# Filler projections placed between the steps of the Gram products of a hybrid encoder on one Trainium2 core

## Chip, core and metric

The kernel runs on one core of one Trainium2 chip. Its time is the device time of one execution in microseconds (us). TensorE is called PE in the profile, VectorE DVE, ScalarE ACT, GpSimd POOL, and SP is the engine whose queue issues the DMAs.

## What is computed

A trunk of two layers on 1024 tokens of width 1024. The first layer normalises, projects into ten groups of columns, and feeds two mixers: A, a recurrence with decay (RWKV-7) of 8 heads of 64, and B, attention in chunks of 64 over the own and eight previous chunks, also 8 heads. Both are gated, joined and projected back. The second layer is a gated spatial mixing, and a normalisation ends it.

```python
def step(state, inp):                       # mixer A
    r_t, w_t, k_t, v_t, a_t, b_t = inp
    sa = jnp.einsum('bhvk,bhk->bhv', state, a_t)
    state = (state * w_t[:, :, None, :]
             + sa[..., None] * b_t[:, :, None, :]
             + v_t[..., None] * k_t[:, :, None, :])
    y_t = jnp.einsum('bhvk,bhk->bhv', state, r_t)
    return state, y_t
...
s = jnp.einsum('bhqd,bhkd->bhqk', q_blk, kb).astype(jnp.float32) * scale + bias    # mixer B
p = jax.nn.softmax(s, axis=-1)
return jnp.einsum('bhqk,bhkd->bhqd', p.astype(vb.dtype), vb)
...
y_a = rwkv7_mix(p_r, p_k, p_v, p_wd, p_ad, w0, w2, a0, a2, k_k, k_a, r_k, lnx_g, lnx_b)
y_a = y_a * jax.nn.silu(gate_a)
y_b = chunk_attention(q_b, k_b, v_b, att_bias) * jax.nn.silu(gate_b)
return h + jnp.concatenate([y_a, y_b], axis=-1) @ w_out
```

## The kernel before

All products are done in three passes of split numbers (high x high, high x low, low x high; lines 256, 258 and 260), so that the large projections dominate TensorE. One such matmul of 128 x 512 is called a filler here when it is issued through `Fill`.

The program goes through these stages, in order of time:

- Normalisation and the projections of mixer A (to about 265 us). Each ends with the decayed keys and queries stored to DRAM (`ar_d`, `bk_d`, `v_d`).
- The recurrence, in four quarters of 256 tokens, each of four chunks of 64. `stage_a` loads `bk`, `ag` and `uv`, and makes the Gram products: for two chunk groups (`cg`) and two pairs of heads (`pj`) it issues one group of matmuls into two PSUM tiles `psg` (line 713; pool `ps_m`, two buffers), which VectorE masks into `G` and `ag` (line 717), four evacuations for a group. Then `rest` scales `bk` on GpSimd and transposes it (`pst`, line 684) through the same two buffers. `stage_b` solves the triangular blocks, a chain on VectorE with small products `psx` (line 770). `stage_c` runs the state from chunk to chunk (`zz`, `yy`, `us`). `stage_d` normalises the output. The `bk` tile has one buffer, so the next load of it waits for the transposes of the one before.
- The attention of eight heads: `att_a` makes scores, `att_b` transposes the probabilities (`st`), splits them (`ph` on ScalarE, `pl` on VectorE) and multiplies with the values into `po`. A finished half of a pair of heads goes, times its gate, to `yb_d`.
- The second half of the output projection from `yb_d`, and then the second layer.

Fillers run through the recurrence and the attention. `early_steps` are the 16 projections of mixer B (q, k, v, gate for four pairs of heads), 48 matmuls each; behind them come `out_steps`, the half of the output projection that needs mixer A alone, 8 x 2 x 12 matmuls, whose weights `WHL` can only be loaded when the last early one is issued. `fill.pump(n, mark, low)` takes n such matmuls from this one sequence; what is left when the attention has been written runs behind it, by `run(fill.steps)`. The loops of the program set how many are asked for at each place: `QP` ahead of the first `stage_a`, `QB` between the quarters, `QC` in each chunk, `QA` and `FILLS` in the attention.

The order on each engine is set by a scheduler at build time, by priority. A filler has a priority lowered by `low` (400 for `QP` and `QB`), and `mark` only sets that it stands behind a certain instruction:

```python
def pump(self, n, mark, low=None):
    self.mark, self.fresh = mark, True
    with tc.high_priority(offset=-(self.low if low is None else low)):
        for _ in range(n):
            next(self.steps, None)
    self.mark = None
```

The engines' queues then run in that order, each instruction waiting for its own operands.

Of the kernel before, what the change touches and what calls it, by code (L numbers as in the profile page):

```python
# [52 lines left out]
YP = 1  # L53
LATE = 1
NPO = 1
QP = 84
FILLS = [5, 4, 4, 6, 4, 3, 3, 3]
QA = 14
QB = [80, 10, 10, 10]
QC = [[8, 8, 7], [8, 9, 7], [8, 8, 9], [8, 8, 7]]  # L60
W0SCALE = 0.6065306597126334

# [37 lines left out]
def trunk_kernel(  # L100
# [4 lines left out]
    nc = tc.nc  # L105
# [145 lines left out]
    fill = Fill()  # L251
# [131 lines left out]
    def proj_cm(*args, **kw):  # L383
        run(proj_steps(*args, **kw))
# [41 lines left out]
    def gate_evac(dst):  # L426

        def evac(ps, hf):
            gt = fl.tile([P, 2, 512], F32, tag="gt", name="gt", bufs=2)
            nc.scalar.activation(gt[:, 0], ps, AF.Tanh, scale=0.5)  # L430
            nc.vector.scalar_tensor_tensor(gt[:, 1], gt[:, 0], 1.0, ps, op0=ALU.add, op1=ALU.mult)
            nc.sync.dma_start(dst[:, hf * 512:hf * 512 + 512], gt[:, 1])
        return evac
# [105 lines left out]
    for p in range(NPAIR):  # L539
# [23 lines left out]
        for hf in range(2):  # L563
# [33 lines left out]
            bk = ra.tile([P, 8, P], F32, tag="bk", name="bk", bufs=2)  # L597
# [66 lines left out]
    hss = [slice(64 * h, 64 * h + 64) for h in range(2)]  # L664
    oss = hss[::-1]

    def stage_a(q):

        d = quart[q]
        d["ag"], d["g"], d["bt"], d["uv"] = [], [], [], []  # L670
        rq = (re_, rb)[q % 2]
        parts = []

        def rest(cg, bk, bt):

            c0 = 4 * q + 2 * cg
            for i in range(2):
                nc.gpsimd.tensor_tensor(
                    bk[:, :, i, :], bk[:, :, i, :], pcs[:, c0 + i, :].unsqueeze(2).to_broadcast([P, 4, P]), op=ALU.mult)
            for pj in range(2):  # L680
                pst = ps_m.tile([P, 4, P], F32, tag="m", name="pst")
                for j in range(2):
                    for i in range(2):
                        nc.tensor.transpose(pst[:, 2 * j + i], bk[:, 2 * pj + j, i, :], ident)
                nc.scalar.copy(bt[:, 2 * pj:2 * pj + 2].rearrange("p j i t -> p (j i) t"), pst)

        for cg in range(2):
            o = 4 * q + 2 * cg
            uv = rq.tile([P, 2, 4, P], F32, tag="uv", name="uv", bufs=2)

            ag = rq.tile([P, 2, 4, 2, P], F32, tag="ag", name="ag", bufs=2)
            bk = (rb if q == 0 and cg else re_).tile(
                [P, 4, 2, P], F32, tag="bt" if q == 0 and cg else "bk", name="bk", bufs=2 if q == 0 and cg else 1)
            nc.sync.dma_start(bk, bk_d[o // 8][:, :, o % 8:o % 8 + 2, :].rearrange("a p c t -> p a c t"))
            for h in range(2):
                nc.sync.dma_start(ag[hss[h], h], ar_d[o // 8][:, hss[h], o % 8:o % 8 + 2, :].rearrange("a p c t -> p a c t"))
            for i in range(2):
                for h in range(2):
                    nc.sync.dma_start(
                        uv[oss[h], i, :, hss[h]],  # L700
                        v_d[o // 8][:, 64 * (o % 8 + i):64 * (o % 8 + i) + 64, hss[h]].rearrange("a s n -> s a n"))
                    if q == cg == i == 0:
                        nc.gpsimd.memset(uv[hss[h], i, :, hss[h]], 0.0)
            if cg == 0:
                d["G"] = rq.tile([P, 2, 4, 2, P], F32, tag="G", name="G", bufs=1)
            g = d["G"][:, cg]
            bt = rq.tile([P, 4, 2, P], F32, tag="bt", name="bt", bufs=2)
            for pj in range(2):
                psg = [ps_m.tile([P, 4, P], F32, tag="m", name=f"psg{h}") for h in range(2)]
                for j in range(2):  # L710
                    for i in range(2):
                        for h in range(2):
                            nc.tensor.matmul(psg[h][:, 2 * j + i], lhsT=bk[hss[h], 2 * pj + j, i, :],  # L713
                                             rhs=ag[hss[h], h, 2 * pj + j, i, :], start=True, stop=True)
                for h in range(2):
                    for dst, r in ((g[:, 2 * pj:2 * pj + 2], hss[h]), (ag[:, h, 2 * pj:2 * pj + 2], oss[h])):
                        nc.vector.tensor_tensor(
                            dst[r].rearrange("p j i t -> p (j i) t"), psg[h][r],
                            gmask[r].unsqueeze(1).to_broadcast([64, 4, P]), op=ALU.mult)
            d["g"].append(g)  # L720
            d["ag"].append(ag)
            d["bt"].append(bt)
            d["uv"].append(uv)
            parts.append((cg, bk, bt))
            if q > 0:
                rest(*parts.pop())
        for a in parts:
            rest(*a)
# [190 lines left out]
    for p in range(NPAIR):  # L919
        proj_cm(w_in_e[0], 1664 + p * P, gate_evac(bg_d[p][1]))  # L920
    fill.pump(QP, mark, FLB)
    stage_a(0)
    mark = stage_b(0)
    stage_a(1)
    fill.pump(QB[0], mark, FLB)
    for q in range(3):
        stage_b(q + 1)
        mark = stage_c(q)
        if q < 2:
            stage_a(q + 2)  # L930
        fill.pump(QB[q + 1], mark, FLB)
        stage_d(q)
# [454 lines left out]
```

## Time and profile before

| | us |
|---|---|
| median of 3 timed runs | 1179.46 (1178.08 to 1182.88) |
| the profiled execution | 1180.27 |
| its span, first to last instruction | 1178.6 |
| TensorE busy | 1119.8 (95%) |
| VectorE, ScalarE, GpSimd busy | 622.6, 469.0, 432.0 |
| mean granted clock of TensorE, share of 2.4 GHz | 0.974 |

The busy time of TensorE is modelled from the starts of its matmuls, so a matmul that stands in the array longer than the next one needs shows as overlap, and a TensorE that works slowly also shows as busy. The granted clock says at which of its two levels, 1.2 or 2.4 GHz, it ran.

### The profile page before, as it was taken

The numbers are of one execution on the slowest core, as the hardware profiler recorded it, in microseconds if no ns is written. First come the engines' busy times: TensorE is split into PE (matmuls) and PEld (weight loads), VectorE is DVE, ScalarE is ACT, GpSimd is POOL, SyncE is SP. The second block draws the span as 40 slices with busy tenths as digits, with TensorE's granted clock in tenths as the row PEclk, the third lists the DMA queues.
The fourth block names the chain that finished last, engine by engine and source line by source line (L and its number), as shares of the span: only waits on it lengthen the run. The fifth ranks groups of instructions, "written<-read, shape, count | busy, mean of one in ns | idle before, by whom it ended". The sixth has DMA issues, their size and how long they took to land.

```text
span 1178.6 us, 21117 instructions
## 1 busy us (share of the span) xinstructions
PE 1119.8 (95%) x8162; PEld 929.2 (79%) x8162; DVE 622.6 (53%) x1276; ACT 469.0 (40%) x1008; POOL 432.0 (37%) x448
## 2 busy tenths in 40 slices
PE   8999999998899898999997899899999999999997
PEld 5788778787777676767886778789998888888886
DVE  6455656456585867634687767464100753333433
ACT  5554554430322232312675646234417232231432
POOL 4345545361223433423322463311402464351222
PEclk9999999995999998999999899999999999999999
DMA  6124446469322533293587784862401232122541
GB/s 209 39 81 143 116 117 164 140 205 193 109 83 83 161 101 100 73 215 118 162 227 184 222 264 147 270 216 90 134 10 55 87 110 72 63 88 89 166 133 71
DMA packets 169125, 156.39 MB, mean 133 GB/s; under 512 B 25257, under 2 KB 138562, under 8 KB 168898
## 3 DMA queue, kind: packets, MB, share of 16 engines
q1 hardware_dynamic: 169026, 155.06, 44.9%
q8 instruction: 64, 1.05, 0.4%
q14 instruction: 35, 0.29, 0.1%
HBM read 102.02 MB, written 53.00 MB: 132 GB/s over the span
## 4 chain that ended last, share of the span: by engine, by line
PE 58%; DMA 7%; DVE 5%; ACT 1%; issue 1%; POOL 1%; SPq 0%; DVEq 0%; ACTq 0%; POOLq 0%
PE acc L256 8%; PE acc L258 8%; PE acc L260 8%; PE accv L256 3%; PE accv L260 3%; PE accv L258 3%; PE accu L256 3%; PE accu L260 2%; PE accg L260 2%; PE accu L258 2%; PE accg L258 2%; PE accg L256 2%; PE st L1069 2%; DMA wraw<-in_w_out_e_dram 2%; PE psx L770 1%; PE psg L713 1%
## 5 line engine op out<-in xcount | busy, mean ns | idle before, releaser
L256 PE MATMUL acc<-xH,wh 128*128 128x512 f32 x528 | 214.7, 407 | 1.6 <-DVE rT L422 0.6
L258 PE MATMUL acc<-xL,wh 128*128 128x512 f32 x528 | 213.5, 405 | 0.0
L225 POOL TENSOR_TENSOR wl<-wraw,wh 128x512 fp32r<-128x512 f32 (+1 forms) x106 | 148.9, 1424 | 175.4 <-ACT wh L222 160.0
L260 PE MATMUL acc<-xH,wl 128*128 128x512 f32 x528 | 212.0, 401 | 0.0
L256 PEld LDWEIGHTS acc<-xH,wh 128*128 128x128 f32 x528 | 101.5, 192 | 23.6 <-DVE rT L422 1.0
L258 PEld LDWEIGHTS acc<-xL,wh 128*128 128x128 f32 x528 | 101.2, 192 | 21.2 <-issue 0.9
L260 PEld LDWEIGHTS acc<-xH,wl 128*128 128x128 f32 x528 | 101.0, 191 | 21.2
L256 PE MATMUL acc<-WHL,yh 128*128 128x512 f32 x256 | 101.9, 398 | 4.5 <-DVE res L1142 3.4
L222 ACT CAST wh<-wraw 128x512 fp32r<-128x512 f32 (+1 forms) x102 | 62.7, 653 | 108.5 <-PE acc L258 43.3
L258 PE MATMUL acc<-WHL,yh 128*128 128x512 f32 x256 | 100.8, 394 | 0.0
L260 PE MATMUL acc<-WHL,yl 128*128 128x512 f32 x256 | 100.8, 394 | 0.0
L256 PE MATMUL accv<-wh,xH 128*128 128x256 f32 x256 | 71.7, 283 | 0.0
L258 PE MATMUL accv<-wl,xH 128*128 128x256 f32 x256 | 71.7, 283 | 0.0
L260 PE MATMUL accv<-wh,xL 128*128 128x256 f32 x256 | 71.4, 285 | 0.0
L256 PEld LDWEIGHTS acc<-WHL,yh 128*128 128x128 f32 x256 | 48.4, 189 | 15.6 <-DVE res L1142 4.1
L258 PEld LDWEIGHTS acc<-WHL,yh 128*128 128x128 f32 x256 | 48.3, 189 | 9.6 <-POOL WHL L1114 0.2
L260 PEld LDWEIGHTS acc<-WHL,yl 128*128 128x128 f32 x256 | 48.1, 188 | 9.7
L256 PE MATMUL accu<-xH,wh 128*128 128x512 f32 x128 | 50.5, 395 | 0.0
L260 PE MATMUL accu<-xH,wl 128*128 128x512 f32 x128 | 49.9, 390 | 0.0
L258 PE MATMUL accu<-xL,wh 128*128 128x512 f32 x128 | 49.9, 390 | 0.0
L260 PE MATMUL accg<-xH,wl 128*128 128x512 f32 x128 | 49.9, 389 | 0.0
L256 PE MATMUL accg<-xH,wh 128*128 128x512 f32 x128 | 49.8, 389 | 0.0
(433 smaller groups left out, 2438.0 us busy)
## 6 DMA issues: line engine op xcount, KB each, us to landing
wraw<-in_w_in_e_dram SPq DMA_DIRECT2D x66, 256.0 KB
wraw<-in_w_in_o_dram SPq DMA_DIRECT2D x32, 256.0 KB
xt<-in_x_dram SPq DMA_DIRECT2D x8, 512.0 KB
ar_d<-ar SPq DMA_DIRECT2D x8, 512.0 KB
q_d<-hl SPq DMA_DIRECT2D x8, 512.0 KB
bk<-bk_d SPq DMA_DIRECT2D x8, 512.0 KB
ag<-ar_d SPq DMA_DIRECT2D x16, 256.0 KB
k_d<-hl SPq DMA_DIRECT2D x8, 512.0 KB
```

What stands on the lines that cost most here:

```text
L222: c_ = hi(wh[:, ks], raw)
L225: nc.gpsimd.tensor_tensor(wl[:, ks], raw, f32(wh[:, ks]), op=ALU.subtract)
L256: fill(nc.tensor.matmul(ps, lhsT=ah(k), rhs=bh(k), start=(k == 0), stop=False), k == 0)
L258: fill(nc.tensor.matmul(ps, lhsT=ah(k), rhs=bl(k), start=False, stop=False), False)
L260: fill(nc.tensor.matmul(ps, lhsT=al(k), rhs=bh(k), start=False, stop=(k == nk - 1)), False)
L713: nc.tensor.matmul(psg[h][:, 2 * j + i], lhsT=bk[hss[h], 2 * pj + j, i, :], rhs=ag[hss[h], h, 2 * pj + j, i, :], start=True, stop=True)
L770: nc.tensor.matmul(ps[t_, i], lhsT=lhsT(f, i), rhs=rhs[f[0], i], start=True, stop=True)
L1069: nc.tensor.transpose(st[:, o:o + P], pfs[j][:, k0:k0 + P], ident)
```

## The change

Each Gram group is followed by `QG` = 6 fillers at the priority of their place (`low` = 0), behind the last matmul of the group. There are four groups in each of the four `stage_a`. `QP` goes from 84 to 104, and the first of `QB` from 80 to 56. `QC`, `QA` and `FILLS` stay, and so does the sequence from which the fillers come.

```diff
-QP = 84
+QP = 104
+QG = 6
 FILLS = [5, 4, 4, 6, 4, 3, 3, 3]
 QA = 14
-QB = [80, 10, 10, 10]
+QB = [56, 10, 10, 10]
...
-                            nc.tensor.matmul(psg[h][:, 2 * j + i], lhsT=bk[hss[h], 2 * pj + j, i, :],
-                                             rhs=ag[hss[h], h, 2 * pj + j, i, :], start=True, stop=True)
+                            m_ = nc.tensor.matmul(psg[h][:, 2 * j + i], lhsT=bk[hss[h], 2 * pj + j, i, :],
+                                                  rhs=ag[hss[h], h, 2 * pj + j, i, :], start=True, stop=True)
+
+                fill.pump(QG, m_, 0)
```

The first place is TensorE's order at the first Gram stage, the last fillers ahead of it (`acc`) and its first groups, before:

```order
L258 MATMUL acc<-xL,wh 128x512
L260 MATMUL acc<-xH,wl 128x512
L713 MATMUL psg_2566<-ag,bk 128x128 x4
L713 MATMUL psg_2567<-ag,bk 128x128 x4
L713 MATMUL psg_2580<-ag,bk 128x128 x4
L814 MATMUL zz<-uv,ag 64x64
L817 MATMUL yy<-uv,ag 64x64
L713 MATMUL psg_2581<-ag,bk 128x128 x4
```

and of the change, where 20 more `acc` stand ahead of these rows:

```order
L259 MATMUL acc<-xL,wh 128x512
L714 MATMUL psg_2601<-ag,bk 128x128 x4
L714 MATMUL psg_2602<-ag,bk 128x128 x4
L261 MATMUL acc<-xH,wl 128x512
L257 MATMUL acc<-xH,wh 128x512
L259 MATMUL acc<-xL,wh 128x512
L261 MATMUL acc<-xH,wl 128x512
L257 MATMUL acc<-xH,wh 128x512
L259 MATMUL acc<-xL,wh 128x512
L714 MATMUL psg_2621<-ag,bk 128x128 x4
L817 MATMUL zz<-uv,ag 64x64
L820 MATMUL yy<-uv,ag 64x64
```

Six fillers have moved between the first group and the second; 6 and 4 more follow in the same way behind the second and the third.

The second place is TensorE's order where the second Gram stage begins. Before, the first 8 transposes `pst` of the first stage are followed by 17 fillers, 8 more transposes and 19 fillers, of which the last stand here ahead of the second stage's first group:

```order
L256 MATMUL acc<-xH,wh 128x512
L258 MATMUL acc<-xL,wh 128x512
L260 MATMUL acc<-xH,wl 128x512
L713 MATMUL psg_2933<-ag,bk 128x128 x2
L713 MATMUL psg_2934<-ag,bk 128x128 x2
```

and of the change:

```order
L257 MATMUL acc<-xH,wh 128x512
L259 MATMUL acc<-xL,wh 128x512
L685 MATMUL pst<-ident,bk 128x128 x16
L714 MATMUL psg_3004<-ag,bk 128x128
L714 MATMUL psg_3005<-ag,bk 128x128
```

All 16 transposes now stand together, directly ahead of the group, and the fillers stand ahead of them.

The third place is the end of the attention on TensorE, the last products `po` of the last head. Before, fillers (`acc<-WHL`) stand between them, and 49 more behind the last one:

```order
L1074 MATMUL po<-ph,vb 128x384
L1074 MATMUL po<-ph,vb 128x128
L260 MATMUL acc<-WHL,yl 128x512
L256 MATMUL acc<-WHL,yh 128x512
L258 MATMUL acc<-WHL,yh 128x512
L1076 MATMUL po<-pl,vb 128x384
L1076 MATMUL po<-pl,vb 128x128
```

and of the change, where the `acc` that follow are the projection from `yb_d`:

```order
L1077 MATMUL po<-ph,vb 128x384
L1077 MATMUL po<-ph,vb 128x128
L1079 MATMUL po<-pl,vb 128x384
L1079 MATMUL po<-pl,vb 128x128
L257 MATMUL acc<-WHL,yh 128x512
L259 MATMUL acc<-WHL,yh 128x512
```

The last filler of the sequence stands early in the products of the seventh head now.

## Rows read from the trace of the kernel before

**Rows 1.** The page: TensorE's busy time, its slices, and its granted clock in tenths.

```profile
PE 1119.8 (95%) x8162; PEld 929.2 (79%) x8162; DVE 622.6 (53%) x1276; ACT 469.0 (40%) x1008; POOL 432.0 (37%) x448
...
PE   8999999998899898999997899899999999999997
...
PEclk9999999995999998999999899999999999999999
```

**Rows 2.** Stretches: length, then PE, PEld, DVE, ACT, POOL, PEclk, DMA share, GB/s.

```profile
265.00:270.00 5.00, 1.15 (x9) 0.78 (x7) 0.00 (x0) 0.00 (x0) 0.01 (x1) 1.00 1.19 253
270.00:294.00 24.00, 22.75 (x112) 19.49 (x111) 17.25 (x29) 1.23 (x3) 4.08 (x4) 0.50 0.90 186
294.00:334.00 40.00, 36.71 (x583) 29.66 (x581) 26.43 (x53) 13.23 (x26) 10.75 (x12) 0.96 0.28 88
334.00:541.00 207.00, 191.52 (x2934) 150.15 (x2935) 131.54 (x291) 58.50 (x124) 74.55 (x86) 0.96 0.45 125
...
629.00:672.00 43.00, 34.21 (x185) 28.77 (x183) 30.55 (x84) 27.34 (x76) 18.41 (x18) 0.88 0.82 219
...
700.00:723.00 23.00, 20.61 (x119) 17.04 (x117) 16.85 (x47) 13.50 (x38) 10.12 (x10) 1.00 0.62 196
723.00:737.00 14.00, 13.46 (x79) 11.22 (x78) 9.77 (x22) 7.12 (x18) 4.63 (x5) 1.00 0.44 135
737.00:750.00 13.00, 13.00 (x58) 10.42 (x56) 3.46 (x6) 1.07 (x2) 2.54 (x2) 1.00 0.79 256
750.00:755.00 5.00, 1.80 (x9) 1.49 (x9) 2.54 (x2) 2.17 (x3) 4.32 (x2) 1.00 0.46 136
```

**Rows 3.** TensorE's timeline: start, duration, line, tiles, form, count [idle before <-releaser].

```profile
264.56 0.39 PE L256 MATMUL acc<-xH,wh 128*128 128x512 f32 x1
...
265.02 0.39 PE L260 MATMUL acc<-xH,wl 128*128 128x512 f32 x1
269.25 4.93 PE L713 MATMUL psg<-ag,bk 64*128 64x128 f32 x24 [3.85 <-DMA ag<-ar_d]
...
288.05 1.12 PE L684 MATMUL pst<-ident,bk 128*128 128x128 f32 x4 [0.68 <-ACT bt L685]
...
300.55 1.17 PE L713 MATMUL psg<-ag,bk 64*128 64x128 f32 x16
```

**Rows 4.** VectorE's timeline, first and last of 16 evacuations of the first stage.

```profile
270.60 0.68 DVE L717 TENSOR_TENSOR G<-psg,gmask 64x512 f32<-64x512 f32 x1 [6.50 <-PE psg L713]
...
289.04 0.68 DVE L717 TENSOR_TENSOR ag<-psg,gmask 64x512 f32<-64x512 f32 x1
```

**Rows 5.** The chain that ended last: start, us, what.

```profile
319.26 4.30 DMA bk<-bk_d
...
403.06 6.90 DMA bk<-bk_d
...
421.89 0.62 PE zz L814 x16
422.50 0.47 PE yy L817 x16
```

**Rows 6.** Stretches of tile acc alone: PE, PEld, DVE, ACT, PEclk, DMA share, GB/s.

```profile
270.00:294.00 24.00, 5.18 (x12) 4.18 (x13) 0.00 (x0) 0.00 (x0) 0.50 0.90 186
...
700.00:723.00 23.00, 10.88 (x40) 6.60 (x38) 3.44 (x5) 0.00 (x0) 1.00 0.62 196
723.00:737.00 14.00, 7.47 (x26) 4.47 (x27) 1.27 (x2) 0.00 (x0) 1.00 0.44 135
```

**Rows 7.** Timelines of VectorE and TensorE at the end of the attention.

```profile
729.72 0.68 DVE L1083 TENSOR_TENSOR yb<-po,lo 64x512 f32<-64x512 f32 x1
...
735.70 0.39 PE L1076 MATMUL po<-pl,vb 128*128 128x384 f32 x2
...
742.50 0.69 DVE L1127 TENSOR_TENSOR yl<-yraw,yh 128x512 fp32r<-128x512 f32 x1
...
752.46 0.69 DVE L1142 TENSOR_TENSOR res<-acc,res 128x512 f32<-128x512 f32 x1 [7.16 <-DMA res<-in_x_dram]
```

## The prediction

> **What bounds the kernel now.** I read the page first. TensorE is busy 95% of the span, and its digits stand at 8 or 9 in nearly every slice; the granted clock has one bad slice, the tenth [rows 1]. So the time is TensorE's work at full clock plus what it loses to waits and to half clock, and since the change adds and removes no matmul, only the lost part can change. The next view is a table of stretches, cut where the program changes its stage [rows 2]. The reader is to see four things in it. In 265 to 270 TensorE works 1.15 us of 5. In 270 to 294 it looks busy (22.75 of 24), but at clock 0.50. From 294 to 541, the recurrence with its fillers, it stands idle 3.3 + 15.5 us at clock 0.96. And in 629 to 672 it is idle 8.8 us: there the last projection has been issued, and the next kind of filler still waits for its weights.
>
> What happens in 265 to 294 is in the timelines [rows 3, 4]. The last filler starts at 265.02, TensorE waits 3.85 us for the first ag load, and then the Gram products run between VectorE's evacuations: 16 of them, the first at 270.60, the last at 289.04, each 0.68 us. Two PSUM buffers mean that TensorE can be only one pair ahead. It is busy in pieces and at half clock for all of that.
>
> **The first Gram stage.** Prices at full clock: two fillers start 0.46 us apart, so one costs 0.23 us; 16 Gram records take 1.17 us; 16 zz records 0.62 and 16 yy records 0.47 [rows 3, 5]. From 265.4 to 294.0, 28.6 us, TensorE did 64 Gram records (4.7), 32 records of zz and yy (1.1), 8 transposes (two fours of 1.12 at half clock, so 1.1 together at full) and 12 fillers (2.8) [rows 3, 6]: 9.7 us of work, 18.9 lost. After the change 20 fillers (4.6 us) cover the 3.85 us wait. Then the order puts 6, 6 and 4 fillers between the Gram pairs: 3.7 us, beside 4.7 + 1.1 of its own work, is 9.5 us in the 16 x 0.68 = 11 us that VectorE needs. Nothing here should hold the clock down. I leave 3.5 us lost (1.5 of pacing, 2 for the last two PSUM buffers, which VectorE frees only after two transposes of its own). **Gain 15.4 us.** The bounds are 18.9 (nothing lost) and 3.85 (only the load wait goes, the clock stays low).
>
> Of the queues: the fillers taken early are the end of a k projection and most of a v projection, whose weights ACT and POOL split, in both orders, ahead of the first Gram stage; their evacuations, stores and the weight loads behind them move forward with them. SP's order up to the last load of the first stage is the same row for row, so no Gram load is late for that reason; behind it two weight loads and one vb_d store now stand ahead of the reload that comes next.
>
> **What the move uncovers.** The second Gram stage must reload the one bk buffer, which the transposes of the first free. Before, the order has 36 fillers between those transposes and the next Gram pair: 36 x 0.23 = 8.3 us, longer than the reload, which takes 4.30 us in one row and 6.90 in another [rows 5]. After, the 16 transposes stand directly ahead of the next pair, and ahead of the third group of that stage it is so again. TensorE's queue is in order, so nothing passes: each time it waits for the DMA less what is left of the transposes (some 1 us). I take 3.5 us each, **7 us**, nearer the 4.30 row, since the DMA share falls from 0.90 to 0.28 there [rows 2]. Bounds: 0 if VectorE is late anyway, and 13.8 (2 x 6.90).
>
> **The other stages.** The budget of early fillers changes thus: ahead of the first stage 84 to 104; in each of four Gram stages 4 x 6 = 24 new; after the second Gram stage 80 to 56. That is 20 + 96 - 24 = 92 more before the attention, 48 of them in the third and fourth Gram stages, 48 x 0.23 = 11 us, in a stretch that loses 15.5 us idle and, at clock 0.96, some 8 us more (8% of 207 us at half) [rows 2]. If they fall into those waits the stretch stays as long and 11 us of work is done in it for nothing; if the chain of evacuation, solve and state is pushed along by them, nothing is won. I take just over the middle, **6 us gained**; bounds 0 and 11.
>
> **The attention pays.** There are 960 filler steps (16 projections x 48, and 8 x 2 x 12 of the first half of the output projection). Up to the attention 574 were asked for, now 666; the attention asks for 332. Before, 54 were left and ran behind it: that is why 737 to 750 is busy 13 of 13 [rows 2]. After, the fillers end 38 early, and the order confirms it: behind the start of the seventh head's products no filler stands until the last po. TensorE has 92 x 0.23 = 21 us less to do there, but loses cover:
> - Seventh head (700 to 723): 40 fillers (9.2 us) and 2.4 idle leave 11.4 us of its own work. VectorE is busy 16.85, of which 5 adds of 0.69 belong to the fillers: 13.4. Without fillers VectorE and its waits set about 15.5 us. Lost 4 where 2.4 were lost: +2.
> - Last head (723 to 737): 26 fillers (6 us) and 0.5 idle leave 7.5; the chain of transposes, copy, subtract and product needs about 9.5: +1.5.
> - Handover: the last head's first half is added at 729.72; its product with the gate, the store, the reload and the split, 742.50 to 743.2, follow [rows 7]. Some 3 us of these 13.5 I put down to queueing behind other work, so the chain needs about 10, and the second half of the head, 6 us with fillers (to the last po at 735.70), then takes some 4. Six us stay open. Before, the 54 leftovers covered it, and what stayed open was one wait of 3.2 us (750 to 755), for a residual load that blocked VectorE until 752.46 [rows 2, 7]: +2.5 net.
>
> **6 us lost** in sum; bounds 2 (VectorE's own time falls with the fillers' traffic gone) and 16 (the half clock below).
>
> **Sum.** -15.4 + 7 - 6 + 6 = -8.4 us. The profiled execution took 1180.3 us, its span 1178.6; the three timed runs have a median of 1179.46. 1179.5 - 8.4 = **1171 us**, -0.7%.
>
> **The rivals.**
> 1. *All of it is won.* The reload is back in time because VectorE's evacuations are late anyway, and the other stages take their 48 fillers into waits: -18 - 10 + 8 = -20, so 1160. For it: 18.8 us idle between 294 and 541 [rows 2], more than the fillers need. Against it: in the order nothing at all stands between the transposes and the pair that needs the reload.
> 2. *No change.* The start wins only its 3.85 us wait and part of the clock, 8 to 10 us, the reload takes 7 back, and the attention's open end the rest: 1178 to 1181. For it: fillers are only moved, and their work was already done at full speed where it stood (13 of 13 busy).
> 3. *Slower: the uncovered heads fall to half clock.* In 629 to 672, where fillers were short before, the clock is 0.88 with TensorE busy 34 of 43, so mostly it held; but in 270 to 294 it stayed at 0.50 [rows 2]. If the last two heads run at 1.2 GHz, their own 11.4 + 7.5 us become 38 instead of the 25 of my forecast: +13, and the two heads that run short of fillers at the beginning of the attention add 3: 1171 + 16 = 1187. It decides once the low level holds through both of the last heads.
>
> The Trainium skill's page "TensorE: Matmul & The Clock Gate" speaks for the third rival in its section "Why this matters for your kernels": idle gaps between bursts of matmuls bring the array back to half rate, so bursts should follow each other directly. Here 265 to 294 agrees (3.85 us of waiting, then 0.50). By that rule the first stage is cured, and the last heads become the next such place, 1187; the 0.88 of 629 to 672 makes me hold this the less likely.
>
> **How the numbers follow.** About 0.5% (6 us) is what a measurement of this kernel tells from no change. My forecast, by its own terms 1164 to 1179: 0.48. First rival 0.18, second 0.19, third 0.15. Faster: rival 1 and about 0.7 of the forecast, 0.52. Same: the rest of the forecast and most of rival 2, 0.30. Slower: rival 3 and a little of rival 2, 0.18. The range that holds 8 in 10 reaches to most of rival 1 and to the edge of rival 3: 1157 to 1186.
>
> **What would show it.** Right: no wait for ag at 265, clock 1.00 through 270 to 285, a wait of 3 to 5 us of TensorE for bk near 290 and another some 15 us later, no acc row among the last head's products, a gap of 4 to 7 us after the last po, and attention done some 15 us earlier relative to its start. Wrong: low clock still in the first Gram stage (then it is not the gap that sets it); no wait for bk (rival 1); the stretch of the recurrence longer by 10 us (its chain is pushed); or low clock through the last heads (rival 3).

## The result, and the profile after

The changed kernel took 1188.38 us (median of six runs, 1187.12 to 1190.1) against 1179.96 us of the kernel before on the same chip (1178.08 to 1182.88): ratio 1.007, 95% interval 1.0054 to 1.0086. It is slower by 0.7%, where the forecast was 0.7% faster. The profiled execution took 1187.37 us, its span is 1185.7. All line numbers behind the Gram products are 3 higher now.

The page, TensorE's busy time, its slices and its granted clock, to be read against [rows 1]:

```profile
PE 1119.7 (94%) x8162; PEld 924.9 (78%) x8162; DVE 616.4 (52%) x1276; ACT 470.2 (40%) x1008; POOL 432.9 (37%) x448
...
PE   7999999998889989999987999899999999999997
...
PEclk8999999998789989999998999999999999999999
```

The one bad slice of the clock has gone (its 5 is an 8), and two weak ones, 7 and 8, stand behind it. The table of stretches says where (columns as in [rows 2]); the last three rows are the heads that run short of fillers, most of the last two heads, and the handover from the attention to the projection behind it:

```profile
265.00:270.00 5.00, 5.00 (x24) 3.92 (x23) 0.57 (x1) 1.64 (x3) 1.54 (x2) 1.00 1.18 249
270.00:283.00 13.00, 13.00 (x112) 10.56 (x110) 8.99 (x15) 0.00 (x0) 3.02 (x3) 1.00 1.13 211
283.00:300.00 17.00, 10.63 (x48) 8.56 (x47) 12.34 (x29) 3.53 (x6) 2.04 (x2) 0.69 0.64 191
300.00:320.00 20.00, 15.12 (x197) 11.16 (x195) 11.91 (x26) 4.21 (x8) 4.97 (x6) 0.75 0.13 41
320.00:340.00 20.00, 15.80 (x247) 12.88 (x247) 17.18 (x45) 5.28 (x11) 3.28 (x4) 0.83 0.23 73
340.00:358.50 18.50, 18.50 (x439) 14.65 (x438) 6.73 (x11) 6.78 (x15) 5.18 (x8) 1.00 0.25 83
...
600.00:643.00 43.00, 32.95 (x187) 27.20 (x185) 30.33 (x90) 27.46 (x75) 16.94 (x17) 0.92 0.82 210
...
734.00:752.70 18.70, 16.68 (x109) 13.93 (x106) 16.46 (x45) 14.35 (x37) 2.55 (x2) 1.00 0.30 102
752.70:757.00 4.30, 0.54 (x3) 0.30 (x3) 1.03 (x2) 1.37 (x3) 2.53 (x2) 1.00 0.51 151
```

From 265 to 283 TensorE is busy all the time at full clock, where it waited and then ran at half clock before [rows 2]. From 283 to 340 it stands idle 6.4 + 4.9 + 4.2 = 15.5 us, and the clock takes 17 x 0.31 + 20 x 0.25 + 20 x 0.17 = 13.7 us more: 29 us lost (idle time at the low clock, a few us, is counted twice). Before, 265 to 334 lost 22 us, counted in the same way from [rows 2]. So the loss has moved to the right, and has grown.

TensorE's waits between 281 and 350 (engine, tile and line, what it waited for: us in total, times, longest):

```profile
PE pv L899 <- ACT vs L896: 4.0, 1, 4.0
PE psg L714 <- issue: 3.7, 1, 3.7
PE psx L773 <- DVE nbt L755: 3.6, 1, 3.6
PE psg L714 <- DMA bk<-bk_d: 2.3, 1, 2.3
PE pst L685 <- DVE nbt L755: 0.9, 1, 0.9
PE pst L685 <- DVE ag L720: 0.9, 2, 0.6
```

The two waits of `psg`, which end at 296.9 and 311.9, are the two reloads of `bk` that the prediction priced. The profile names the load for the first alone; that the second is one too is read from the second load of `bk`, issued at 308.3, and from e6 below, where both waits are gone. The first and the third row the prediction did not have. Behind the first stands this row of ScalarE's timeline: the evacuation of a value projection found no free buffer until an earlier k projection's store to `k_d` had landed.

```profile
286.51 0.60 ACT L896 ACTIVATE vs<-acc 128x512 f32<-128x512 f32 x1 [17.11 <-DMA k_d<-hl]
```

For the `psx` wait, VectorE's timeline is to be read (start, us, duration). The first solve's `D<-xe` stood at 303.41 before; now evacuations of the second Gram stage stand inside the solve's chain, and four transposes (`nw`) of the second solve ahead of the first solve's copies `D<-psx`:

```profile
309.72 1.04 DVE L763 STREAM_TRANSPOSE D<-xe 128x512 f32<-128x512 f32 x1 [1.03 <-ACT xe L760]
...
324.27 4.35 DVE L744 STREAM_TRANSPOSE nw<-G 32x512 f32<-32x512 f32 x4
...
329.18 0.42 DVE L780 COPY D<-psx 16x256 f32<-16x256 f32 x1
330.61 0.43 DVE L780 COPY D<-psx 16x256 f32<-16x256 f32 x1
```

Two marks carry the rest: the 16 copies `z<-zz` (one for each chunk; the last one ends the recurrence) and the first product of the second layer, `accv`. Each row gives a tile's count, its durations in ns, and its first and last start, before:

```profile
L821 DVE COPY z<-zz x16: 406/425/426, 283.2 to 536.9; 128x256 f32<-128x256 f32 x16
...
L256 PE MATMUL accv<-wh,xH x256: 277/283/387, 787.8 to 893.5; 128*128 128x256 f32 x128
```

and of the change:

```profile
L824 DVE COPY z<-zz x16: 404/424/426, 281.4 to 555.6; 128x256 f32<-128x256 f32 x16
...
L257 PE MATMUL accv<-wh,xH x256: 277/283/387, 794.8 to 900.6; 128*128 128x256 f32 x128
```

So the recurrence ends 18.7 us later, the attention and handover take 239.2 instead of 250.9 us (11.7 less), and the second layer takes 390.8 in both: +7.1.

### The profile page after: what moved, and what is told of

Its sections match the earlier page's. It is cut to its first block, busy times and chain, and to the rows that moved or that the text cites. A ratio compares the mean times of both kernels' runs of the same rounds, so it can differ in the third digit from the quotient of the medians.

```text
span 1185.7 us, 21117 instructions
## 1 busy us (share of the span) xinstructions
PE 1119.7 (94%) x8162; PEld 924.9 (78%) x8162; DVE 616.4 (52%) x1276; ACT 470.2 (40%) x1008; POOL 432.9 (37%) x448
## 4 chain that ended last, share of the span: by engine, by line
PE 77%; DMA 9%; DVE 9%; ACT 2%; issue 2%; SPq 1%; POOL 1%; ACTq 0%; POOLq 0%; DVEq 0%
PE acc L259 13%; PE acc L257 13%; PE acc L261 13%; PE accv L257 3%; PE accv L261 3%; PE accv L259 3%; PE accu L257 3%; PE accu L259 2%; PE accu L261 2%; PE accg L259 2%; PE accg L257 2%; PE accg L261 2%; DMA wraw<-in_w_out_e_dram 2%; PE psg L714 2%; PE psx L773 2%
## 5 line engine op out<-in xcount | busy, mean ns | idle before, releaser
L1075 DVE TENSOR_TENSOR pl<-st,ph 128x512 fp32r<-128x512 f32 (+1 forms) x64 | 41.3, 650 | 19.3 <-ACT ph L1074 18.9
L1117 POOL TENSOR_TENSOR WHL<-wraw,WHL 128x512 fp32r<-128x512 f32 (+1 forms) x20 | 30.2, 1510 | 54.9 <-ACT WHL L1116 54.9
```

What stands on the lines that cost most here:

```text
L1075: nc.vector.tensor_tensor(pl[:, 0:o], st[:, 0:o], f32(ph[:, 0:o]), op=ALU.subtract)
L1117: (lo or (nc.vector if k % 2 else nc.gpsimd)).tensor_tensor(wl, raw, f32(wh), op=ALU.subtract)
```

## The experiments

There were 18. The marks are those of one profiled execution for each kernel (us), which lies up to some 4 us from the kernel's median (e5: 1174.44 against 1178.61), so differences of a few us between marks are not told from noise; "more" is how many fillers were asked for ahead of the attention beyond the kernel before; "solve" is the time from the first `nb` (the first solve begins) to the first `us`. Ratio is to the kernel before on the same chip, with its 95% interval. The expectations call fillers projections, and their 164, 208, 212 and 256 count `QP`, `QB[0]` and the Gram stages alone.

| kernel | more | ratio | solve | 2nd z | 16th z | last po | 2nd layer |
|---|---|---|---|---|---|---|---|
| before | 0 | | 37.4 | 340.5 | 536.9 | 735.9 | 787.8 |
| e1_ahead | 0 | 0.9992 (0.9974 to 1.0011) | 38.4 | 341.9 | 540.4 | 736.7 | 787.8 |
| e2_first | 0 | 1.0011 (0.9995 to 1.0028) | 31.6 | 338.5 | 540.1 | 737.0 | 788.3 |
| e17_place_only | 6 | 1.0108 (1.0080 to 1.0136) | 45.8 | 350.9 | 548.1 | 744.3 | 799.7 |
| e13_plain24 | 24 | 1.0019 (1.0002 to 1.0035) | 37.5 | 342.3 | 539.9 | 740.6 | 786.7 |
| e9_plain44 | 44 | 0.9944 (0.9925 to 0.9963) | 37.2 | 343.2 | 541.2 | 737.7 | 781.9 |
| e3_early2 | 44 | 0.9928 (0.9907 to 0.9950) | 52.4 | 356.3 | 535.9 | 733.2 | 775.2 |
| e8_early2_bk | 44 | 0.9968 (0.9950 to 0.9987) | 50.8 | 357.3 | 539.4 | 737.5 | 780.7 |
| e18_half | 44 | 1.0006 (0.9989 to 1.0024) | 50.0 | 354.9 | 544.7 | 741.0 | 784.0 |
| e4_late2 | 48 | 0.9931 (0.9908 to 0.9954) | 37.1 | 342.5 | 538.5 | 739.7 | 780.2 |
| e12_ahead_late | 48 | 0.9962 (0.9944 to 0.9981) | 38.3 | 336.1 | 536.5 | 737.6 | 778.6 |
| e5_supply | 48 | 1.0004 (0.9987 to 1.0021) | 46.8 | 349.4 | 543.7 | 741.2 | 781.6 |
| e14_plain68 | 68 | 1.0051 (1.0030 to 1.0072) | 37.2 | 341.8 | 545.9 | 747.3 | 792.7 |
| e11_three | 68 | 1.0124 (1.0100 to 1.0148) | 53.6 | 357.6 | 551.2 | 751.1 | 798.2 |
| e10_plain92 | 92 | 1.0026 (1.0007 to 1.0046) | 38.0 | 342.3 | 548.1 | 745.9 | 789.8 |
| changed | 92 | 1.0070 (1.0054 to 1.0086) | 55.8 | 358.5 | 555.6 | 752.7 | 794.8 |
| e7_kd | 92 | 1.0076 (1.0050 to 1.0103) | 51.4 | 356.1 | 555.3 | 751.8 | 795.0 |
| e15_early2_plain48 | 92 | 1.0088 (1.0069 to 1.0107) | 55.6 | 359.0 | 553.8 | 753.0 | 795.5 |
| e16_fills | 92 | 1.0099 (1.0080 to 1.0118) | 55.8 | 358.8 | 555.7 | 746.9 | 794.8 |
| e6_bk | 92 | 1.0122 (1.0088 to 1.0155) | 49.6 | 354.3 | 552.8 | 754.0 | 795.2 |

The first theory was that the second Gram stage, carried ahead of the first solve, costs the time; its rival, that the attention lacks the 92.

**e1_ahead** (diffs from here on are against the changed kernel, unless another is named)

```diff
-QG = 6
+QG = 0
-QB = [56, 10, 10, 10]
+QB = [60, 10, 10, 10]
```

> Only the 20 projections more ahead of the first Gram product; none between its steps; as many projections ahead of attention as before (164). Theory 1 (the time is lost because projections at the place of the second Gram stage carry that stage ahead of the first solve): the second Gram stage stays behind, the first chunk's z copy comes 2 to 5 us after that of the changed kernel (281.4), the second's by 342 (358.5 in the changed kernel), 1170 to 1177 us. Theory 2 (the time is lost at the end, since attention has 92 projections fewer): nothing is taken from attention, so 1170 to 1177 too. Theory 3 (the first Gram stage's gain is given back whatever follows): 1178 to 1182.

**e2_first**

```diff
-QB = [56, 10, 10, 10]
+QB = [36, 10, 10, 10]
-                fill.pump(QG, m_, 0)
+                fill.pump(QG if q == 0 else 0, m_, 0)
```

> The 20 ahead, and six between the steps of the first Gram stage alone, not of the second, third and fourth; 164 ahead of attention as before. Theory 1: z of the second chunk by 342, 1165 to 1174 us. Theory 2: the same, 1165 to 1174. Theory 3: 1178 to 1186, with z of the second chunk past 350, because the projections of the first stage alone already bring the value projection, on which TensorE waited 4.0 us at 283.

No change in either: 1178.03 and 1180.29 us are the third theory's times (its mark for e2, a second z copy past 350, did not come: 338.5). e2 is the prediction's first term by itself: TensorE is busy 18.0 of 18 us from 265 to 283 at clock 1.00, the wait is gone, and the kernel takes as long as before. What was won comes back behind it:

```profile
270.00:283.00 13.00, 13.00 (x104) 10.16 (x103) 9.14 (x14) 0.61 (x2) 4.23 (x4) 1.00 1.19 209
283.00:300.00 17.00, 12.00 (x66) 10.03 (x65) 13.63 (x27) 4.85 (x9) 4.55 (x4) 0.90 0.74 209
300.00:340.00 40.00, 35.51 (x612) 29.54 (x611) 31.61 (x68) 10.99 (x22) 8.20 (x11) 0.83 0.24 72
```

From 300 to 340 the clock is 0.83 and 4.5 us are idle: the fillers issued early are missing in the solve (40 between its first `nb` and the first `us`, 80 before). The solve itself is shorter (31.6 us against 37.4); the second z copy is 2.0 us earlier than before, and the 16th is 3.2 us later, so more is given back behind 340.

**e3_early2**

```diff
-                fill.pump(QG, m_, 0)
+                fill.pump(QG if q < 2 else 0, m_, 0)
```

> The 20 ahead, and six between the steps of the first and the second Gram stage, none in the third and fourth; 208 projections ahead of attention (before 164, changed kernel 256). Theory 1: the second chunk's z copy at 358 as in the changed kernel, and without the 11 us that the 48 projections of later stages cover but with 44 of them back in attention (about 4 us): 1186 to 1196 us. Theory 2: half of what attention lost is back, 1176 to 1184.

**e4_late2**

```diff
-QP = 104
+QP = 84
-QB = [56, 10, 10, 10]
+QB = [80, 10, 10, 10]
-                fill.pump(QG, m_, 0)
+                fill.pump(QG if q > 1 else 0, m_, 0)
```

> None of the 20 ahead, none in the first and second Gram stage, six between the steps of the third and fourth; 212 projections ahead of attention. Theory 1: the second chunk's z copy at 340 as before, the 48 are taken in by waits that are there (11 us), attention pays 4 to 5 us for 48 fewer: 1170 to 1176 us. Theory 2: attention pays for 48 of 92, 1180 to 1186 us.

Both are 0.7% faster than before, though each holds half of the change. e3 has the second z copy at 356.3, nearly as late as in the change, and is as fast as any kernel here (1169.95 us; both theories had it slower), so a late second chunk does not decide the time by itself, and the first theory fell. In e4, theory 1's 1170 to 1176 us held (1171.17), and theory 2's 1180 to 1186 did not.

The next four try the supply of the attention, and the two kinds of wait at 283 to 312. **e5_supply**

```diff
-QB = [56, 10, 10, 10]
+QB = [12, 10, 10, 10]
```

> The changed kernel with 12 instead of 56 projections behind the second stage: six between the steps in all four Gram stages stay, but 212 instead of 256 projections go ahead of attention. Theory 1 (supply: only 49 projections stood uncovered behind the last head, and each one moved beyond them is taken from a wait inside attention): attention and the handover lose 8 us less than in the changed kernel, five projections or so are left for the handover, 1168 to 1176 us. Theory 2 (place: six at all four stages lengthen the chunks' chain, as the step of 34.5 us between the eighth and ninth z copy): the z copies keep their times, 1180 to 1187 us.

**e6_bk**, and **e8_early2_bk** with the same edit on e3

```diff
-            bk = (rb if q == 0 and cg else re_).tile(
-                [P, 4, 2, P], F32, tag="bt" if q == 0 and cg else "bk", name="bk", bufs=2 if q == 0 and cg else 1)
+            alt = q + cg == 1
+            bk = (rb if alt else re_).tile(
+                [P, 4, 2, P], F32, tag="bt" if alt else "bk", name="bk", bufs=2 if alt else 1)
```

> The changed kernel, where the second stage's first bk tile goes into a buffer that is free (a bt buffer of the other pool), so that neither reload of bk waits for the other's transposes. Theory 1 (the two reload waits, 6.0 us idle, and the low clock behind them lengthen the first solve): no wait for bk at 295 and 308, the second z copy 8 to 14 us earlier than 358.5, 1176 to 1183 us. Theory 2 (VectorE's queue, in which the second solve's transposes stand ahead of the first solve's copies, sets the second z copy): it moves by under 4 us, 1185 to 1190 us.

> The 20 ahead and six between the steps of the first and second Gram stage alone (208 ahead of attention), and the second stage's first bk in a free buffer. Theory 1 (reload waits): 6 to 12 us faster than without the buffer, 1158 to 1164 us. Theory 2 (VectorE's queue sets the second z copy): 1167 to 1171 us, as without it.

**e7_kd**

```diff
-            nc.sync.dma_start(dst[:, :, hf * 512:hf * 512 + 512].rearrange("x p t -> p x t"), f32(hl))
+            nc.gpsimd.dma_start(dst[:, :, hf * 512:hf * 512 + 512].rearrange("x p t -> p x t"), f32(hl))
```

> The changed kernel, where the stores of q and k (q_d, k_d) are issued by GpSimd and not behind SyncE's loads, so that the buffer for the value projection's vs comes free earlier. Theory 1 (the wait of 4.0 us for vs and the low clock behind it are lost time on the path): no wait at 283, the first nb at 288 to 290 instead of 291.9, 1182 to 1187 us. Theory 2 (the reload of bk and the solve take up whatever is won there): nb earlier, but the second z copy within 2 us of 358.5, 1187 to 1190 us.

e5 fell between its theories (1178.61). e6 and e7 took their waits away and won nothing. e6 (1191.21 us) missed both its ranges, and is slower than the change (1.0122 against 1.0070). e7 (1187.41) has the change's time, but its first `nb` came at 293.9 and not earlier, as both its theories had it. e8 (1174.82) missed both its ranges, and was 4 parts in 1000 slower than e3. In e6 no `psg` waits for a load any more (waits of TensorE, 281 to 343, the two longest), and a `psx` waits instead, on ScalarE's queue:

```profile
PE psx L774 <- ACT hl L888: 5.8, 1, 5.8
PE pv L900 <- ACT vs L897: 4.4, 1, 4.4
```

In e7 the wait of `pv` is gone, and TensorE waits longer for the two reloads:

```profile
PE psg L714 <- DMA bk<-bk_d: 7.2, 2, 3.6
PE psx L773 <- DVE nbt L755: 3.6, 1, 3.6
```

The second z copy moved by 4.2 and 2.4 us, and the 16th by 2.8 and 0.3. Neither of these waits carries the loss by itself: the one that is taken away is followed by the next.

**e9_plain44** and **e10_plain92** separate the number of fillers from their place: nothing at the Gram stages, `QB` of the kernel before raised (diffs against before). e9:

```diff
-QB = [80, 10, 10, 10]
+QB = [80, 24, 25, 25]
```

> The kernel before with 44 projections more ahead of attention, all at lowest priority behind the first three rounds of chunks (24, 25 and 25 in place of 10, 10 and 10); nothing ahead of or between the Gram products. Theory 1 (number: the waits of the chunk stages have room for some 46 projections more, wherever they are put, and 49 stood uncovered behind the last head): the last z copy at 535 to 541, 1168 to 1173 us, as with the 44 at the first two Gram stages and the 48 at the last two. Theory 2 (place: only projections between the Gram steps fill waits): the last z copy 8 to 10 us later than before's 536.9, 1177 to 1182 us.

e10:

```diff
-QB = [80, 10, 10, 10]
+QB = [80, 40, 41, 41]
```

> The kernel before with 92 projections more ahead of attention at lowest priority (40, 41 and 41 in place of 10, 10 and 10), as many as the change moves, none ahead of or between the Gram products. Theory 1 (number): 46 of them find no wait, the last z copy is past 547, attention is short of them, 1180 to 1190 us. Theory 2 (place: the change loses by where it puts them, in the first and third solve): 1166 to 1176 us.

The number's theory held twice: with 44 at lowest priority the kernel is as fast as e4 and nearly as e3, with 92 it is slightly slower than before. Rows of the z copies and of the second layer's first product, e9:

```profile
L821 DVE COPY z<-zz x16: 405/424/425, 286.0 to 541.2; 128x256 f32<-128x256 f32 x16
...
L256 PE MATMUL accv<-wh,xH x256: 277/283/387, 781.9 to 887.7; 128*128 128x256 f32 x128
```

and of e10:

```profile
L821 DVE COPY z<-zz x16: 404/424/425, 284.3 to 548.1; 128x256 f32<-128x256 f32 x16
...
L256 PE MATMUL accv<-wh,xH x256: 277/283/387, 789.8 to 895.6; 128*128 128x256 f32 x128
```

**e11_three**

```diff
-                fill.pump(QG, m_, 0)
+                fill.pump(QG if q < 3 else 0, m_, 0)
```

> The changed kernel without the 24 projections of the fourth Gram stage (68 more ahead of attention than before instead of 92). Theory 1 (number): between the 44 and the 92, 1174 to 1182 us. Theory 2 (place: the fourth stage's projections stand in the third solve, and make the step of 34.5 us between the eighth and ninth z copy): that step 15 to 22 us, 1168 to 1174 us.

**e12_ahead_late**, against e4

```diff
-QP = 84
+QP = 104
-QB = [80, 10, 10, 10]
+QB = [60, 10, 10, 10]
```

> The 20 ahead of the first Gram product (taken from those behind the second stage), none in the first two Gram stages, six between the steps of the third and fourth: 48 more ahead of attention than before. Theory 1 (number): as with the 48 alone, 1168 to 1173 us; what the 20 win at the first stage comes back as waits in the first solve. Theory 2 (place: gains of places add up): 5 us faster than the 48 alone, 1162 to 1167 us.

e11 (1193.77 us) missed both: it is slower than the change with 24 fewer, though the step from the eighth to the ninth z copy shrank from 34.5 to 26.4 us. e12 is 1 us above the number's range; the 20 ahead add nothing to e4.

**e13_plain24** and **e14_plain68**, against the kernel before (e14 with 32, 33, 33)

```diff
-QB = [80, 10, 10, 10]
+QB = [80, 18, 18, 18]
```

> The kernel before with 24 projections more ahead of attention at lowest priority (18 in place of 10 behind each of three rounds). Number: all 24 come out of the 49 that stood uncovered behind the last head (5.5 us) and find room in waits: 1173 to 1177 us. If the gain of the 44 needs their place in the later rounds, no change: 1177 to 1181.

> The kernel before with 68 projections more at lowest priority (32, 33 and 33 behind the three rounds). Number: 49 of them are a gain, 19 come out of attention for nothing, 1174 to 1178 us. If the place at three Gram stages was not what made the run with 68 there slow (1.0124 of before), this one is slow as well: 1188 us or more.

**e15_early2_plain48**, against e3

```diff
-QB = [56, 10, 10, 10]
+QB = [56, 26, 26, 26]
```

> The 20 ahead and six between the steps of the first two Gram stages, and 48 more at lowest priority behind the later rounds instead of six in the third and fourth Gram stage: 92 more than before, as in the change. If the change's cost over the 92 at lowest priority lies in the last two Gram stages: the last z copy at 546 to 550, 1177 to 1182 us. If it lies in the first two (second z copy 18 us late): 1185 to 1190 us.

**e16_fills**

```diff
-FILLS = [5, 4, 4, 6, 4, 3, 3, 3]
+FILLS = [5, 4, 4, 4, 3, 3, 3, 3]
```

> The changed kernel, with fewer projections issued at each step of the fourth and fifth head (4 and 3 instead of 6 and 4), so that heads seven and eight, which had 2 and 0, have some. If want of them in the last heads costs the time (low clock, gap behind the last product): 3 to 6 us faster than the changed kernel, 1182 to 1185 us. If they are worth the same in any head, as their sum in attention is fixed: 1186 to 1190 us.

e13 and e14 were both slower than the number's forecast: e13 shows no gain (1178.52, the other expectation's range), e14 is 6 us above (1183.76), though well short of e11, and so between its two expectations. e15 is as slow as the change, so the two later stages are not what sets the change apart from e10. In e16 the attention ended 5.8 us earlier (746.9), and the second layer began at the same 794.8: one wait behind the last `po` took it all (TensorE, 745 to 758):

```profile
PE acc L257 <- ACT yh L1129: 8.9, 1, 8.9
```

The chain there runs through the store of a late filler's result, GpSimd's gate and the reload (start, us):

```profile
745.12 2.31 DMA hp_d<-res
747.53 1.27 POOL gb L1095
748.86 1.27 POOL yb L1096
...
752.46 2.91 DMA yraw<-yb_d
```

**e17_place_only** and **e18_half** keep all of the change's places, with nearly the number of before, and with 44. e17:

```diff
-QB = [56, 10, 10, 10]
+QB = [0, 0, 0, 0]
```

> The changed kernel with none of the projections behind the second stage and behind the rounds of chunks (0, 0, 0, 0 in place of 56, 10, 10, 10): all of the change's places, but 6 more ahead of attention than before instead of 92. If number decides and place costs nothing by itself: 1174 to 1180 us. If the place costs 5 to 8 us by itself: 1182 to 1187 us, with the last z copy past 541.

e18:

```diff
-QG = 6
+QG = 3
```

> The changed kernel with three instead of six projections behind each group of the Gram stages: 44 more ahead of attention than before. If number decides: 1169 to 1174 us, like the other kernels with 44 to 48. If the place costs 5 to 8 us by itself: 1175 to 1181 us.

The places cost time at a like number: e17 takes 1192.61 us, 12.8 more than before, past its expected range, with the last z copy 11.2 us late. Its first solve takes 45.8 us with 32 fillers in it, where before it took 37.4 with 80, and in e2 31.6 with 40. So it is not the fillers in it that make it long, nor the want of them, but its own chain has grown:

```profile
293.20:339.00 45.80, 9.89 (x32) 6.14 (x32) 0.00 (x0) 0.59 (x1) 0.83 0.20 63
```

(fillers alone, columns as in [rows 6]). e18 is 7 us slower than e9 by the ratios, with the same number.

## Why the prediction was wrong

Set against the marks, the prediction was: recurrence +6.6 us (21 us of fillers more, less 15.4, plus 7, less 6), attention and handover -15 (21 less, 6 of cover lost). Measured: +18.7 and -11.7.

**"Gain 15.4 us" in the first Gram stage: this step failed.** Locally it came true (no wait for `ag`, clock 1.00 until 283). But it was counted as time off the end. e2, which makes this edit and leaves the number alone, took 1.0011 of the time before; e1, which makes the first half of it, 0.9992. What TensorE lost there was not what the next stage waited for: the first solve (`nb`) begins when VectorE has masked and transposed. Before:

```profile
289.76 2.13 DVE L741 STREAM_TRANSPOSE nw<-G 32x512 f32<-32x512 f32 x2
292.00 0.48 DVE L744 SCALAR_TENSOR_TENSOR nb<-nw,half 128x256 f32<-128x256 f32 x1
```

and of the change:

```profile
286.95 0.68 DVE L720 TENSOR_TENSOR ag<-psg,gmask 64x512 f32<-64x512 f32 x1
288.99 0.69 DVE L902 TENSOR_TENSOR vv<-pv,vv 128x512 fp32r<-128x512 f32 x1 [1.35 <-ACT vv L901]
289.71 2.12 DVE L744 STREAM_TRANSPOSE nw<-G 32x512 f32<-32x512 f32 x2
291.94 0.48 DVE L747 SCALAR_TENSOR_TENSOR nb<-nw,half 128x256 f32<-128x256 f32 x1
```

The first Gram product starts at 269.65 (269.25 before), for fillers fill the wait for the load and do not shorten it. VectorE's 16 evacuations, priced at 11 us, take 16.7 in the change (19.1 before), with 2.1 us of transposes and 3.0 us of waits for TensorE between them. So they end 2.1 us earlier, at 287.6, and the add `vv<-pv` of the value projection that moved forward, with the wait before it, takes these; `pv` is what TensorE waited 4.0 us for. In e2 `nb` starts at 293.6, 1.6 us later than before. And the fillers that close the gap in e1 and e2 are taken from the solve. In e12 and e18 the solve did begin earlier (287.3, 288.2); their medians are no better than those of e4 and e9, which move the same numbers, though e12's profiled execution ends its recurrence 2.0 us before e4's.

**"What the move uncovers", 7 us: mis-sized, and more than the reload.** The two reload waits came 15 us apart, as predicted, and measured 2.3 + 3.7 = 6.0. But each came with a stretch of half clock behind it, and the term had idle time alone (columns as in [rows 2]):

```profile
297.00:303.00 6.00, 6.00 (x28) 4.74 (x29) 3.77 (x9) 0.00 (x0) 0.00 (x0) 0.50 0.01 1
311.00:317.00 6.00, 5.07 (x100) 4.04 (x101) 3.17 (x5) 1.29 (x3) 0.59 (x1) 0.51 0.03 11
```

The waits for `pv` and `psx` have such stretches behind them too (0.50 in 286.8 to 293, 0.52 in 331.5 to 337.5). In all, 283 to 340 lost 15.5 us idle and 13.7 to the clock. Nor is the reload the cause of the late second chunk: without it (e6) the second z copy was only 4.2 us earlier. What is shown is the place: in all kernels with fillers inside the second Gram stage the first solve takes 45.8 to 55.8 us, in all without 31.6 to 38.4. That VectorE's queue is how (the second stage's evacuations and transposes ahead of the first solve's) is read from the timeline and was not tried by itself. The order that I had compared showed the second stage drawn together, and I priced only the load that it waits for, not the solve that it passes.

**"6 us gained" in the other stages: near.** By the rows' count the start lost some 7 us more (29 against 22), so of the recurrence's +18.7, less 21 of work, some 9 us were regained behind it. At lowest priority the 92 cost the recurrence 11.2 us (e10), at the change's places 18.7.

**"The attention pays", 6 us: 9 measured** (21 less work, 11.7 us won), most of it not where the step had it. A head has 24 products `po`, so the last two heads begin at 700.92 before and at 729.66 in the change, and the last one there at 742.77. Products `acc` alone (columns as in [rows 6]), before:

```profile
700.92:736.10 35.18, 17.07 (x60) 10.35 (x61) 4.05 (x6) 0.00 (x0) 1.00 0.53 168
```

and of the change:

```profile
729.66:752.90 23.24, 0.68 (x2) 0.30 (x2) 0.69 (x1) 0.00 (x0) 1.00 0.34 112
742.77:752.90 10.13, 0.00 (x0) 0.00 (x0) 0.00 (x0) 0.00 (x0) 1.00 0.14 52
```

With 58 fillers (13.2 us) fewer the last two heads are 11.9 us shorter: 1.3 us lost, where the prediction had 3.5. The last head takes 10.1 us without fillers (predicted: about 9.5). Behind the last `po` 9.8 us are won with 49 fillers (11.1 us) fewer: 1.3 lost, where it had 2.5; the gap there is 3.8 us, just under its 4 to 7. The rest, some 7 us, is lost ahead of the seventh head, a term that the forecast had at nothing (the third rival had 3 us for it): from the last z copy to that head it takes 174.0 us with 315 fillers, 164.0 before with 301. The starved heads (600 to 643, TensorE idle 10 us) come earlier there, as the early projections run out earlier. From the last z copy to the last `po` the time is 196 to 201 us in nearly every kernel, with 317 fillers in it as with 360; only e16 has 191.2, and gives it back.

**The number.** Before, 49 fillers ran behind the last `po`. An estimate from the rows is that those alone are worth 0.23 us each when moved, and that in the recurrence each costs some 0.12 at lowest priority (11.2 us for 92). This fits a gain at 44 (e9) and none at 92 (e10). It doesn't fit e13, with no gain at 24, nor e14, which by it would gain 3 us with 68 and is 0.5% slower than before: attention and handover take 246.8 us there, and 240.7 and 241.7 in e9 and e10. So single steps of the order matter by some us too.

**The rivals.** The third one's time came out (1187 against 1188.38), but by luck: its mechanism did not, as both last heads ran at clock 1.00. The second one's reason, that the start wins little, is what e1 and e2 show, at its 1178 to 1181 us; for the change its time was too low. The first one's 1160 is far off. The Trainium skill's page "TensorE: Matmul & The Clock Gate", section "Why this matters for your kernels", has idle gaps between bursts of matmuls bring the array back to half rate. The trace of the change agrees in 283 to 340 (waits of 2.3 to 4.0 us, clock 0.69 to 0.83). That sentence of the page doesn't tell e1 from e12 (below), where TensorE's order is one and the clock two.

**Open.** Why six fillers at the first two stages (e3) or the last two (e4) cost nothing, while three or four stages cost 2 to 11 us in the last z copy against a like number at lowest priority (e5, e18, e11, the change, e17; the 2 of e5 is within the noise of a mark), and why the first two cost as much once 92 are moved (e15). That the change is slower by its places as well as by its number is shown (e10, e17); how the places do it is not: none of the waits tried explains it, and each kernel has another order on every engine.

## What to carry to other kernels

Filling a gap on the busiest engine gained nothing here by itself (e2). Ask first what the next stage waits for, and take the work from a place where it stands uncovered (here the 49 fillers behind the last product). Moving 44 to 48 gained 0.3 to 0.7% in five of seven kernels; 24 gained nothing, and 68 and 92 lost. Work at lowest priority did nearly as well as work put into the gap by hand (e9 and e3), and left the running solve as long as before (37.2 us in e9). When a wait is priced, price the half clock behind it too, and ask what the stage that moves up will pass on the other engines.

## What the runs showed of the hardware

The order of TensorE, VectorE, ScalarE and GpSimd is the same in e1 and e12 until 370 us, well past the first `us`. The clock still differed. The same stretch in e1:

```profile
265.00:283.00 18.00, 17.15 (x100) 14.49 (x100) 7.73 (x12) 1.64 (x3) 5.45 (x7) 0.75 1.13 231
```

and in e12:

```profile
265.00:283.00 18.00, 15.69 (x124) 13.05 (x124) 11.94 (x18) 2.22 (x4) 6.62 (x7) 0.99 1.17 225
```

TensorE's longest wait in it was 0.85 us in e1 and 1.11 us in e12, at 273 in both; behind it the clock of 274 to 283 was 0.50 in e1, and that of 273 to 283 was 0.98 in e12. The first solve began at 292.9 us in the one and at 287.3 in the other. So the same order of small bursts kept its clock in one execution and lost it in another; the two ran on different chips, and whether the chip or chance decides isn't shown. Here that is worth 5.6 us, as much as most of the differences in the table, which is why single executions don't decide between them.
